# A two-layer decoder trunk on one core: one triangular substitution for two groups of heads, and a new order of steps in the first mixer

## The chip, the core and the metric

The kernel runs on one core of a Trainium2 chip. The core has a matrix engine (TensorE, PE in the profile), a vector engine (VectorE, DVE), a scalar engine (ScalarE, ACT), a general one (GpSimd, POOL) and a queue engine (SyncE, SP) that here only issues DMA transfers. Each engine works through its own instructions in the order in which the built program has them; between engines, semaphores order the work. The metric is the device time of one execution in microseconds (us), lower is better. The kernel before takes 1161.52 us, the median of three runs (1161.10 to 1162.86).

## What is computed

512 tokens of width 1024 go through two layers, each a mixer, a layer norm, a squared-ReLU MLP and a second layer norm. The change lies in the mixer of the first layer:

```python
def mixer_a(h, mem, w_in, conv_w, A_log, dt_bias, norm_w, mem_w_kv, w_o):
    proj = h @ w_in                                  # q, k, v, z, a, b, qm
    qkv = jax.nn.silu(causal_depthwise_conv(qkv, conv_w))
    q, k = l2_normalize(...), l2_normalize(...)      # 6 heads of 128
    o = gated_delta_rule(q, k, v, g, beta)
    o = o * lax.rsqrt(jnp.mean(o * o, axis=-1, keepdims=True) + NORM_EPS) * norm_w
    o = o * jax.nn.silu(z)
    mo = memory_cross_attention(qm, mem, mem_w_kv)   # 4 heads, 256 memory tokens
    return jnp.concatenate([o, mo], axis=-1) @ w_o

def gated_delta_rule(q, k, v, g, beta):              # by chunks of tokens
    L = jnp.where(strict, (k_beta @ k.T) * decay, 0)
    u, w = triangular_solve(I + L, [v * beta, k_beta * exp(g)])
    for each chunk:
        v_new = u - w @ state
        out = q_dec @ state + intra @ v_new
        state = state * chunk_decay + k_dec.T @ v_new
```

## The kernel before

All products are float32 with the operands split into a high and a low part, three matrix products for one (L105 to L107 with the weights as the stationary operand, L118 to L122 with the tokens). A weight slab comes in by one DMA on the SP queue (`wr`, three buffers), ACT casts its high part (L87, `wh`), DVE subtracts for the low part (L88, `wl`); four buffers each.

The six heads form two **groups** of three. The kernel uses chunks of 128 tokens, so a group has 12 units (three heads by four chunks). For each head, k and q are projected (step k, L105), go through the convolution (ACT L385, three DVE instructions L387, ACT's silu L389); then `ak` (L414) makes k·k and k·q, and DVE scales these into `LT` (L427, the triangular matrix) and E (L429, the attention inside a chunk). E's decay matrix is made beforehand by step E from two tiles `y`, one made by DVE and one by POOL (L375).

The inverse of each 128x128 unit triangle is made in two stages. **The substitution** (step i, `inv_blocks`): the 32x32 diagonal blocks of a group's 12 units are gathered through DRAM (`dl` four DMAs, `ld` one), so that 48 partitions hold one block each. 31 steps of two DVE instructions (L483 product `tmp`, L485 subtraction into `X`) invert them all at once; `X` goes back through DRAM (`dx`, then `TT` in four DMAs). **The join** (step j, `inv_join`): DVE transposes TT into `U` (L496), and two levels of small products (32x32: ipp, ip; 64x64: iqp, iq), with copies on ACT and DVE between them, fill the off-diagonal blocks. This is done once per group.

**v** (steps v and w): projection, convolution, then PE transposes (`vt` L459) and DVE scales into `vr` (L460). **z**: step z projects all four token tiles of a column slab (`proj_zMM`), step n applies silu (ACT L686), and POOL multiplies in the norm's weight (L688, 128x768). **The memory's attention** (step m) for one token tile: scores `msc`, DVE's maximum (L619), ACT's exp (L624), transposes `mpt`, copies `pT` (into the buffers named y, which E and the convolutions use too), values `mov`.

**The scan** (step c, `group_chunk`): for one chunk and group kt (transposed k, ACT scales into kd L546), ks and qs (the state with k and q), R on DVE (L555), tr (U times R), vn on ACT (L563), ds (the new state), od, o (ACT L581, DVE L582). Step o (`chunk_out`) squares o on ACT (L592) and multiplies into z. Step f turns a finished token tile into features (L676 to L679), W loads and p applies the output weights (`wo`).

What sets the order: a list of steps, written by hand, is run in this sequence (a letter is the step, digits its arguments; c12 is group 1, chunk 2):

```python
MIXER_ORDER = """q0 g1 g0 E0 k02 k01 k00 E1 k12 i0 k10 k11 q1 z1 m3 v00 i1 m1 w00 v01 j0 m0 v02 w01 m2 z0 w02 M c00 v10 n0 o00
c01 n1 v11 w10 o01 c02 n2 o02 j1 c03 v12 w11 w12 c10 n3 W1 W0 o03 o10 c11 f0 o11 c12 o12 f1 W3 c13 p10 p00 o13
p01 f3 f2 X p11 p02 p12 p03 W2 p23 p20 p30 p32 p31 L0 p21 p13 p22 L1 L2 p33 L3"""
```

A scheduler then lays the instructions of all engines out from it, so that neighbouring steps are interleaved; `behind` puts one instruction behind another on the same engine without a semaphore. The rest of the program (both MLPs, the second layer) comes after and is not touched.

Of the kernel before, what the change touches and what calls it, by code (L numbers as in the profile page):

```python
# [11 lines left out]
F32 = mybir.dt.float32  # L12
# [11 lines left out]
NH = 6  # L24
# [10 lines left out]
MIXER_ORDER = """q0 g1 g0 E0 k02 k01 k00 E1 k12 i0 k10 k11 q1 z1 m3 v00 i1 m1 w00 v01 j0 m0 v02 w01 m2 z0 w02 M c00 v10 n0 o00  # L35
c01 n1 v11 w10 o01 c02 n2 o02 j1 c03 v12 w11 w12 c10 n3 W1 W0 o03 o10 c11 f0 o11 c12 o12 f1 W3 c13 p10 p00 o13
p01 f3 f2 X p11 p02 p12 p03 W2 p23 p20 p30 p32 p31 L0 p21 p13 p22 L1 L2 p33 L3"""
# [12 lines left out]
def trunk(ctx: ExitStack, tc: tile.TileContext, xT, xn, memT, wk, wq, wv, wqm, wz, wmk, wmv, wo0, wo1, up, dn,  # L50
          bw, ws, conv, alog, dtb, nw, sinks, lng, lnb, lngb, pos, invf, out):
    nc = tc.nc
    V, G, A, T, SY = nc.vector, nc.gpsimd, nc.scalar, nc.tensor, nc.sync
# [47 lines left out]
    def feature_major(ps, w, mov_hi, mov_lo):  # L101
        hi, lo = w
        for k in range(KT):
            mh, ml = mov_hi(k), mov_lo(k)
            T.matmul(ps, hi[:, k, :], mh, start=(k == 0), stop=False)  # L105
            T.matmul(ps, hi[:, k, :], ml, start=False, stop=False)
            T.matmul(ps, lo[:, k, :], mh, start=False, stop=(k == KT - 1))  # L107
# [150 lines left out]
    nw_b = row_bcast(nw, P, "nw_b", c0)  # L258
# [34 lines left out]
    def proj_z(zg, gates=None, slabs=None):  # L293

        slabs = slabs or [wload(wz[zg, kh], [P, 4, CW]) for kh in range(2)]
        c0 = zg * CW
        n = min(CW, 768 - c0)
        for t in range(NT):
            ps = mmt("proj_zMM")
            token_major(ps[:, :CW], slabs, x_tok(XH, t), x_tok(XL, t))  # L300
            A.copy(res[:, t, c0:c0 + n], ps[:, :n])
            if gates is not None:
                V.tensor_copy(gates[:, :, t], ps[:, n:n + 12])

    ab = c0([P, 12, NT], "ab")
    slabs = [w[1]() for w in zw]
    for t in range(1, NT):
        xs[t][1](XH[:, :, tok(t)], XL[:, :, tok(t)])
    proj_z(2, ab, slabs)
# [57 lines left out]
    def make_E1(gi):  # L367
        E1 = dt_([P, NU, P], "E1")
        for hl in range(GH):
            h = GH * gi + hl  # L370
            ps = smt("E1")
            psv = ps.rearrange("p (c i) -> p c i", c=4)
            for i, eng in enumerate((V, G)):
                gm = dt_([P, 4, P], "y", dt=F32R)
                eng.tensor_tensor(gm, triu[:, :].unsqueeze(1).broadcast_to([P, 4, P]),  # L375
                                  fr(gsp[i])[:, h * 4:h * 4 + 4].unsqueeze(2).broadcast_to([P, 4, P]), op=ALU.mult)
                T.matmul(ps, slow, gm.rearrange("p c i -> p (c i)"), start=(i == 0), stop=(i == 1))
            dst = E1[:, hl * 4:hl * 4 + 4, :]
            V.tensor_tensor(dst, psv, mtri[:, :].unsqueeze(1).broadcast_to([P, 4, P]), op=ALU.add)
            A.activation(dst, dst, AF.Exp)  # L380
        E1s[gi] = E1

    def conv_silu(ps, ch, dst):
        y = dt_([P, 512], "y")
        A.activation(y, ps, AF.Identity, scale=convw[:, ch, 3:4])  # L385
        for s in (1, 2, 3):
            V.scalar_tensor_tensor(y[:, s:], ps[:, :512 - s], convw[:, ch, 3 - s:4 - s], y[:, s:],  # L387
                                   op0=ALU.mult, op1=ALU.add)
        A.activation(dst, y.rearrange("p (c i) -> p c i", c=4), AF.Silu)  # L389
# [10 lines left out]
    def group_kq(gi, hl):  # L400
# [5 lines left out]
        for which, (wsrc, chb) in enumerate(((wk, 6), (wq, 0))):  # L406
# [3 lines left out]
        ak = [smt("ak").rearrange("p (u i) -> p u i", u=2) for _ in range(2)]  # L410
        ss = dt_([P, 8], "ss")
        junk = dt_([P, P], "junk", bufs=1)
        for c in range(4):
            T.matmul(ak[c // 2][:, c % 2, :], kq[:, hl, c, 0, :], kq[:, hl, c, :, :], start=True, stop=True)  # L414
            V.tensor_tensor_reduce(junk, ak[c // 2][:, c % 2, 0:P], ident, 1.0, 0.0, op0=ALU.mult, op1=ALU.add,
# [8 lines left out]
        for c in range(4):  # L424
            u = hl * 4 + c
            akc = ak[c // 2][:, c % 2, :]
            V.scalar_tensor_tensor(LT[:, u, :], akc[:, 0:P], g["s1"][:, u:u + 1], E1[:, u, :],  # L427
                                   op0=ALU.mult, op1=ALU.mult)
            V.scalar_tensor_tensor(E1[:, u, :], akc[:, P:2 * P], g["rk"][:, u:u + 1], E1[:, u, :],  # L429
                                   op0=ALU.mult, op1=ALU.mult)  # L430
# [12 lines left out]
    def group_v(gi, hl):  # L443
# [5 lines left out]
        conv_silu(ps, 12 + h, g["vt", hl])  # L449

    def group_v2(gi, hl):
        g = groups[gi]
        vt = g["vt", hl]
        if "vr" not in g:
            g["vr"] = dt_([P, GH, 4, P], ("vr", "TT0")[gi], bufs=1)
# [4 lines left out]
        V.tensor_tensor(g["vr"][:, hl], ptv, g["rinv"][:, hl * 4:hl * 4 + 4].unsqueeze(2).broadcast_to([P, 4, P]),  # L460
# [4 lines left out]
    def inv_blocks(gi):  # L465

        LT = groups[gi]["LT"]
        dl = drp.tile([4, NU, 32, 32], F32, tag="dl", name=nm("dl"))
        for b in range(4):
            q = slice(32 * b, 32 * b + 32)  # L470
            SY.dma_start(dl[b].rearrange("u j i -> j u i"), LT[q, :, q])
        ld = dt_([Q, 32, 32], "ld", bufs=1)
        SY.dma_start(ld.rearrange("q j i -> q (j i)"), dl.rearrange("b u j i -> (b u) (j i)"))
        X = dt_([Q, 32, 32], "X", bufs=1)
        G.memset(X, 0.0)
        G.memset(X.rearrange("q i m -> q (i m)")[:, 0:1024:33], 1.0)
        tmp = dt_([Q, 256], "tmp", bufs=1)
        TT = groups[gi]["TT"] = dt_([P, NU, P], f"TT{gi}", bufs=1)
        G.memset(TT, 0.0)
        for j in range(31):  # L480
            n, m = 31 - j, j + 1
            tv = tmp[:, 0:n * m].rearrange("q (i m) -> q i m", m=m)
            V.tensor_tensor(tv, ld[:, j, j + 1:32].unsqueeze(2).broadcast_to([Q, n, m]),  # L483
                            X[:, j, 0:m].unsqueeze(1).broadcast_to([Q, n, m]), op=ALU.mult)
            V.tensor_sub(X[:, j + 1:32, 0:m], X[:, j + 1:32, 0:m], tv)  # L485
        dx = drp.tile([4, NU, 32, 32], F32, tag="dx", name=nm("dx"))
        SY.dma_start(dx.rearrange("b u i m -> (b u) (i m)"), X.rearrange("q i m -> q (i m)"))
        for b in range(4):
            q = slice(32 * b, 32 * b + 32)
            SY.dma_start(TT[q, :, q], dx[b].rearrange("u i m -> i u m"))  # L490

    def inv_join(gi):
        g = groups[gi]
        LT, TT = g["LT"], g["TT"]
        U = g["U"] = dt_([P, NU, P], "U")
        V.transpose(U.rearrange("p u i -> p (u i)"), TT.rearrange("p u i -> p (u i)"))  # L496

        b0, b1, b2, b3 = (slice(32 * b, 32 * b + 32) for b in range(4))
        pp = smt("ipp")[:, 0:NU * 32].rearrange("p (u i) -> p u i", u=NU)
        for u in range(NU):  # L500
            T.matmul(pp[b1, u, :], LT[b0, u, b1], TT[b0, u, b0], start=True, stop=True)
            T.matmul(pp[b3, u, :], LT[b2, u, b3], TT[b2, u, b2], start=True, stop=True)
        Pf = dt_([P, NU, 32], "Pf")
        A.copy(Pf[b1], pp[b1])
        V.tensor_copy(Pf[b3], pp[b3])
        p2 = smt("ip2")[:, 0:NU * 32].rearrange("p (u i) -> p u i", u=NU)
        p3 = smt("ip3")[:, 0:NU * 32].rearrange("p (u i) -> p u i", u=NU)
        for u in range(NU):
            T.matmul(p3[b1, u, :], U[b1, u, b1], Pf[b1, u, :], start=True, stop=True)
        for u in range(NU):  # L510
# [848 lines left out]
```

## Time and profile before

| | |
|---|---|
| median of three runs | 1161.52 us |
| the profiled execution | 1161.59 us, of it 1159.9 us span |
| instructions on the span | 19009 |
| PE, DVE, ACT, POOL busy | 1135.8, 861.0, 555.4, 237.3 us |
| the first mixer's projections to the end of its scan | about 50 to 270 us of the span |

Busy time of an engine is the union of its instructions. A matmul in the profile has a modelled end, so that matmuls which follow each other overlap: how fast PE really works is read from the distance of their starts.

### The profile page before, as it was taken

The numbers are of one execution on the slowest core, as the hardware profiler recorded it, in microseconds if no ns is written. First come the engines' busy times: TensorE is split into PE (matmuls) and PEld (weight loads), VectorE is DVE, ScalarE is ACT, GpSimd is POOL, SyncE is SP. The second block draws the span as 40 slices with busy tenths as digits, with TensorE's granted clock in tenths as the row PEclk, the third lists the DMA queues.
The fourth block names the chain that finished last, engine by engine and source line by source line (L and its number), as shares of the span: only waits on it lengthen the run. The fifth ranks groups of instructions, "written<-read, shape, count | busy, mean of one in ns | idle before, by whom it ended". The sixth has DMA issues, their size and how long they took to land.

```text
span 1159.9 us, 19009 instructions
## 1 busy us (share of the span) xinstructions
PE 1135.8 (98%) x7494; PEld 1000.2 (86%) x7494; DVE 861.0 (74%) x1612; ACT 555.4 (48%) x1010; POOL 237.3 (20%) x178
## 2 busy tenths in 40 slices
PE   9999999989999999999999999999999999999997
PEld 9887788879998899898988887778989898989986
DVE  5678889867798766667675968886987667676657
ACT  6445354755484445444443336661655444444531
POOL 1202111110014332424220100000042324233203
PEclk9999999999999999999999999999999999999999
DMA  8523041204323233242323241102333242322311
GB/s 297 163 74 89 34 137 38 68 20 158 129 76 126 94 98 121 73 135 84 122 96 107 63 140 56 56 20 73 110 118 119 75 137 81 124 95 91 128 37 73
DMA packets 41017, 114.17 MB, mean 98 GB/s; under 512 B 11168, under 2 KB 12064, under 8 KB 40928
## 3 DMA queue, kind: packets, MB, share of 16 engines
q1 hardware_dynamic: 40496, 112.17, 29.6%
q8 instruction: 59, 0.97, 0.3%
q10 hardware_dynamic: 432, 0.79, 0.2%
q14 instruction: 30, 0.25, 0.1%
HBM read 109.53 MB, written 3.41 MB: 97 GB/s over the span
## 4 chain that ended last, share of the span: by engine, by line
PE 81%; DVE 13%; ACT 3%; issue 1%; POOL 1%; DMA 0%; SPq 0%; DVEq 0%; ACTq 0%; POOLq 0%
PE dn L121 10%; PE dn L122 10%; PE dn L118 10%; PE upb L949 3%; PE upb L951 3%; PE upb L950 3%; PE wo L122 2%; PE wo L118 2%; PE wo L121 2%; PE upd L951 2%; PE upd L950 2%; PE upd L949 2%; PE upa L950 2%; PE upa L951 2%; PE upa L949 2%; DVE y L387 2%
## 5 line engine op out<-in xcount | busy, mean ns | idle before, releaser
L87 ACT CAST wh<-wr 128x1024 fp32r<-128x1024 f32 (+1 forms) x126 | 132.2, 1052 | 213.0 <-PE dn L122 153.2
L88 DVE TENSOR_TENSOR wl<-wr,wh 128x1024 fp32r<-128x1024 f32 (+1 forms) x126 | 153.9, 1224 | 65.2 <-ACT wh L87 64.8
L118 PE MATMUL dn<-wh,hh 128*128 128x512 f32 (+1 forms) x516 | 200.3, 388 | 0.0
L122 PE MATMUL dn<-wh,hl 128*128 128x512 f32 (+1 forms) x516 | 200.3, 388 | 0.0
L121 PE MATMUL dn<-wl,hh 128*128 128x512 f32 (+1 forms) x516 | 200.2, 388 | 0.0
L122 PEld LDWEIGHTS dn<-wh,hl 128*128 128x128 f32 x516 | 96.9, 188 | 19.9
L121 PEld LDWEIGHTS dn<-wl,hh 128*128 128x128 f32 x516 | 97.0, 188 | 18.9
L118 PEld LDWEIGHTS dn<-wh,hh 128*128 128x128 f32 x516 | 97.0, 188 | 18.8
L1030 DVE TENSOR_TENSOR res<-res,dn 128x512 f32<-128x512 f32 (+1 forms) x121 | 82.0, 678 | 40.9 <-PE dn L122 40.8
L939 POOL TENSOR_TENSOR sa<-wr 128x512 f32<-128x512 f32 x26 | 35.5, 1367 | 353.7 <-DMA wr<-in_up_dram 326.3
L728 POOL TENSOR_TENSOR rs<-rs,nhalf 128x1 f32<-128x1 f32 x16 | 12.8, 799 | 324.7 <-DVE rs L727 271.3
L949 PE MATMUL upb<-TH,wh 128*128 128x256 f32 x208 | 57.6, 277 | 1.6 <-DVE u L988 1.6
L950 PE MATMUL upa<-XL,wh 128*128 128x256 f32 x208 | 57.7, 278 | 0.0
L940 POOL TENSOR_TENSOR sb<-sa,wr 128x512 f32<-128x512 f32 x26 | 57.7, 2220 | 0.0
L951 PE MATMUL upa<-XH,wl 128*128 128x256 f32 x208 | 57.6, 277 | 0.0
L127 DVE TENSOR_TENSOR hl<-r,hh 128x1024 fp32r<-128x1024 f32 x26 | 56.1, 2159 | 1.9 <-ACT hh L126 1.9
L951 PE MATMUL upd<-XH,wl 128*128 128x256 f32 x208 | 57.5, 276 | 0.0
L951 PE MATMUL upb<-TH,wl 128*128 128x256 f32 x208 | 57.5, 276 | 0.0
L949 PE MATMUL upd<-XH,wh 128*128 128x256 f32 x208 | 57.5, 276 | 0.0
L950 PE MATMUL upb<-TL,wh 128*128 128x256 f32 x208 | 57.5, 276 | 0.0
L950 PE MATMUL upd<-XL,wh 128*128 128x256 f32 x208 | 57.5, 276 | 0.0
L126 ACT CAST wh<-wr 128x1024 fp32r<-128x1024 f32 x26 | 27.4, 1054 | 53.6 <-PE upa L950 53.6
(410 smaller groups left out, 3314.9 us busy)
## 6 DMA issues: line engine op xcount, KB each, us to landing
wr<-in_up_dram SPq DMA_DIRECT2D x64, 512.0 KB, 4.4
wr<-in_dn_dram SPq DMA_DIRECT2D x64, 512.0 KB, 4.4
wr<-in_wo_dram SPq DMA_DIRECT2D x16, 512.0 KB, 3.7
wr<-in_bw_dram SPq DMA_DIRECT2D x8, 512.0 KB, 4.2
wr<-in_wk_dram SPq DMA_DIRECT2D x6, 512.0 KB, 3.7
wr<-in_wq_dram SPq DMA_DIRECT2D x6, 512.0 KB, 4.1
wr<-in_wv_dram SPq DMA_DIRECT2D x6, 512.0 KB, 3.7
wr<-in_wz_dram SPq DMA_DIRECT2D x4, 520.0 KB, 4.4
```

Of the source, the lines that this page charges most:

```text
L87: A.copy(hi, raw)
L88: V.tensor_sub(lo, raw, fr(hi))
L118: mm = T.matmul(ps, sh, hi[:, kk, :], start=(k == 0), stop=False)
L121: T.matmul(ps, sh, lo[:, kk, :], start=False, stop=False)
L122: last = T.matmul(ps, sl, hi[:, kk, :], start=False, stop=(k == nk - 1))
L127: return V.tensor_sub(lo, src, fr(hi))
L939: G.tensor_tensor(sa[:, 0], raw[1][:, kA], raw[1][:, kB], op=ALU.add)
L940: G.tensor_tensor(sb[:, 0], sa[:, 0], raw[0][:, kA], op=ALU.subtract)
L949: T.matmul(ps, hi[:, k, :], m, start=start and k == 0, stop=False, skip_group_check=True)
L950: T.matmul(ps, hi[:, k, :], ml[:, k, :], start=False, stop=False, skip_group_check=True)
L951: T.matmul(ps, lo[:, k, :], mh[:, k, :], start=False, stop=stop and k == 3, skip_group_check=True)
L1030: V.tensor_tensor(dst, dst, ps, op=ALU.add)
```

## The change

1. The substitution runs once for both groups: 96 partitions, 31 steps. Each head's blocks are gathered as soon as that head's `LT` exists (`inv_gather`, step i with two digits, four DMAs a head), each group's into its half of `ld`; step I is the substitution, J the two transposes into U, j the join of both groups, whose levels alternate between the groups. The second copy of `Pf` moves from DVE to ACT.
2. `ak` is two products: k·k after k's projection and q·k after q's.
3. The memory's attention is three steps (m scores, t turn, u values) and stands among the projections of k and q; both qm projections come first. `pT` uses the buffer of X.
4. z is projected one token tile at a time (step y), after the slab's load (step z); the norm's weight is no longer multiplied by POOL (L688 goes) but as a scale on ACT and DVE where a finished tile is turned into features.
5. The scan's step c ends with vn, and d (`group_state`) does the rest, so that the chunks of both groups alternate. The squares of a chunk stand behind the next chunk's vn, and f behind the next R.
6. The convolutions of v's heads 3 and 4 stand behind the last substitution step, that of head 5 behind the transposes into U.

```diff
-MIXER_ORDER = """q0 g1 g0 E0 k02 k01 k00 E1 k12 i0 k10 k11 q1 z1 m3 v00 i1 m1 w00 v01 j0 m0 v02 w01 m2 z0 w02 M c00 v10 n0 o00
...
+MIXER_ORDER = """E02 g0 q0 g1 q1 E01 k02 i02 m0 t0 E12 E00 k01 u0 k12 i12 m1 t1 i01 m2 k00 E11 t2 u1 i00 E10 m3 k10 t3
+u2 i10 u3 k11 v00 w00 i11 v01 v02 w01 z1 I y10 z0 y11 J y12 y13 w02 y00 y01 v10 v11 n0 v12 w10 y03 y02 j w11 c00 w12 n1
+c10 d00 d10 c01 n2 W1 d01 c11 W0 d11 o00 o10 c02 c12 n3 d12 f0 d02 o01 o11 p10 W3 c03 o02 f1 c13 p11 d03 d13 o12 p00 f2
...
-        conv_silu(ps, 12 + h, g["vt", hl])
+        conv_silu(ps, 12 + h, g["vt", hl], None if h < 3 else diag["last"] if h < 5 else diag["U"])
...
+    def inv_gather(gi, hl):
...
+            SY.dma_start(dl[b, u4].rearrange("u j i -> j u i"), g["LT"][q, u4, q])
+        g["moved"] += 1
+        if g["moved"] == GH:
+            SY.dma_start(diag["ld"][gi * Q:gi * Q + Q].rearrange("q j i -> q (j i)"),
+                         dl.rearrange("b u j i -> (b u) (j i)"))
...
-            V.tensor_tensor(tv, ld[:, j, j + 1:32].unsqueeze(2).broadcast_to([Q, n, m]),
-                            X[:, j, 0:m].unsqueeze(1).broadcast_to([Q, n, m]), op=ALU.mult)
-            V.tensor_sub(X[:, j + 1:32, 0:m], X[:, j + 1:32, 0:m], tv)
...
+            V.tensor_tensor(tv, ld[:, j, j + 1:32].unsqueeze(2).broadcast_to([2 * Q, n, m]),
+                            X[:, j, 0:m].unsqueeze(1).broadcast_to([2 * Q, n, m]), op=ALU.mult)
+            diag["last"] = V.tensor_sub(X[:, j + 1:32, 0:m], X[:, j + 1:32, 0:m], tv)
...
+        for f, i in ((lower, 0), (lower, 1), (upper, 0), (lower, 2), (upper, 1), (lower, 3), (upper, 2), (upper, 3)):
+            f(i)
...
+    def group_state(gi, c):
...
+        if c:
+            qs = v3(smt("qs"))
             for hl in H:
                 T.matmul(qs[:, hl, :], kq[:, hl, c, 1, :], St[:, hl, :], start=True, stop=True)
...
-            A.activation(junk, o[:, hl, :], AF.Square, accum_out=sso[:, hl:hl + 1])
+            behind(A.activation(junk, o[:, hl, :], AF.Square, accum_out=sso[:, hl:hl + 1]), g.get(("vn", c + 1)))
...
-        zv = res[:, t, 0:768].rearrange("p (h d) -> p h d", h=NH)
-        G.tensor_tensor(zv, zv, nw_b[:, :].unsqueeze(1).broadcast_to([P, NH, P]), op=ALU.mult)
...
-        to_features(res[:, t, :], t)
+
+        for j in range(2):
+            features_half(res[:, t, :], t, j, nw_c, 4 - 2 * j, mmt)
```

What this makes of the order is seen in three places. The first is DVE where group 1's substitution begins in the kernel before (tmp and X are the substitution, y a head's convolution, v its projection, mx the maximum of the attention's scores, wl a weight's low part):

```order
331 L485 TENSOR_TENSOR X_1215<-X_1215,tmp_1218 48x31
332 L88 TENSOR_TENSOR wl_2119<-wr_2116,wh_2118 128x1040
333 L387 SCALAR_TENSOR_TENSOR y_1714<-v_1682,convw,y_1714 128x511
334 L619 TENSOR_REDUCE mx_1807<-msc_1801 128x2
335 L387 SCALAR_TENSOR_TENSOR y_1714<-v_1682,convw,y_1714 128x510
336 L619 TENSOR_REDUCE mx_1807<-msc_1802 128x2
337 L387 SCALAR_TENSOR_TENSOR y_1714<-v_1682,convw,y_1714 128x509
338 L620 TENSOR_SCALAR mx_1807<-mx_1807 128x4
339 L483 TENSOR_TENSOR tmp_1730<-ld_1725,X_1727 48x31
340 L485 TENSOR_TENSOR X_1727<-X_1727,tmp_1730 48x31
```

In the changed kernel DVE comes to the one substitution here (L539 and L541 are its two lines, L416 the convolution, L109 a weight's low part):

```order
253 L416 SCALAR_TENSOR_TENSOR y_1712<-v_1680,convw,y_1712 128x509
254 L481 SCALAR_TENSOR_TENSOR rq_74_703<-ss_1604 128x4
255 L482 TENSOR_SCALAR rqs_704<-ss_1604 128x4
256 L539 TENSOR_TENSOR tmp_1827<-ld_865,X_1824 96x31
257 L506 TENSOR_TENSOR vr_1718<-vt_1719,rinv_658 128x512
258 L541 TENSOR_TENSOR X_1824<-X_1824,tmp_1827 96x31
259 L109 TENSOR_TENSOR wl_1933<-wr_1930,wh_1932 128x1040
260 L416 SCALAR_TENSOR_TENSOR y_1762<-v_1730,convw,y_1762 128x511
```

The maxima are gone from this place, and the first substitution step, which waits for `ld`, now has a weight's subtraction and the convolution of the second v head (`v_1730`) right behind it.

The second is SP's queue in the changed kernel, where the last heads' blocks are gathered (`dl_1167` is group 1's DRAM tile, `ld_865` the tile that the substitution reads):

```order
53 L521 DMA dl_1167<-LT_76_705 32x4x32 x4
54 L105 DMA wr_1936<-in_wz_dram 128x1040
55 L521 DMA dl_1167<-LT_76_705 32x4x32 x4
56 L105 DMA wr_2083<-in_wv_dram 128x1024
57 L524 DMA ld_865<-dl_1167 48x1024
58 L105 DMA wr_2121<-in_wv_dram 128x1024
```

In the kernel before it stands so, for group 0:

```order
43 L471 DMA dl_1208<-LT_72_695 32x12x32 x4
44 L84 DMA wr_1555<-in_wz_dram 128x1040
45 L473 DMA ld_1213<-dl_1208 48x1024
46 L84 DMA wr_1683<-in_wv_dram 128x1024
```

Both put one weight load between the gather and `ld`; the gather that counts is now that of one head instead of a whole group.

The third is PE at the end of the join. Before, for group 1 (v is the last head's projection, the rows below it group 0's last chunk and v's transposes):

```order
1176 L521 MATMUL iqp_2573<-TT_225_1731,LT_63_686 64x64 x6
1177 L105 MATMUL v_2633<-XH,wh_2636 128x512
1178 L106 MATMUL v_2633<-XL,wh_2636 128x512
1179 L107 MATMUL v_2633<-XH,wl_2637 128x512
1180 L526 MATMUL iq_350_2582<-U_2502,Pf_2580 64x64 x6
1181 L521 MATMUL iqp_2590<-TT_225_1731,LT_63_686 64x64 x6
1182 L526 MATMUL iq_353_2599<-U_2502,Pf_2597 64x64 x6
1183 L553 MATMUL ks_2607<-S_2268,kq_687 128x128 x3
1184 L558 MATMUL qs_2608<-S_2268,kq_687 128x128 x3
```

In the changed kernel, for both groups, and on into the first chunks:

```order
1040 L69 MATMUL iq_318_2413<-U_1968,Pf_2402 64x64 x6
1041 L69 MATMUL iqp_2421<-TT_266_1830,LT_76_705 64x64 x6
1042 L69 MATMUL iq_321_2430<-U_1968,Pf_2411 64x64 x6
1043 L69 MATMUL iqp_2438<-TT_266_1830,LT_76_705 64x64 x6
1044 L69 MATMUL iq_324_2447<-U_1970,Pf_2428 64x64 x6
1045 L69 MATMUL iq_325_2455<-U_1970,Pf_2445 64x64 x6
1046 L72 MATMUL vt_2463<-ident,vt_2151 128x128 x4
1047 L72 MATMUL kt_2471<-ident,kq_656 128x128 x3
1048 L69 MATMUL tr_2478<-vr_1718,U_1968 128x128 x3
1049 L72 MATMUL vt_2485<-ident,vt_2190 128x128 x4
1050 L72 MATMUL kt_2494<-ident,kq_697 128x128 x3
1051 L69 MATMUL tr_2501<-X_2197,U_1970 128x128 x2
```

No projection stands among the join's products any more, and the first chunks of both groups follow at once; the first output-weight products come two chunk pairs later.

282 lines of the change are left out of this document (171 added, 111 removed).

## The prediction, as put on record

> **What bounds the kernel now.** First the page's busy times, then its chain of work:
>
> ```profile
> PE 1135.8 (98%) x7494; PEld 1000.2 (86%) x7494; DVE 861.0 (74%) x1612; ACT 555.4 (48%) x1010; POOL 237.3 (20%) x178
> ...
> PE 81%; DVE 13%; ACT 3%; issue 1%; POOL 1%; DMA 0%; SPq 0%; DVEq 0%; ACTq 0%; POOLq 0%
> ```
>
> PE is the bound, and its matmuls stay as they are but for details. So only two things can be won: time in which PE has nothing to start, and time at a lower clock. Two neighbouring starts from PE's timeline give the pace:
>
> ```profile
> 60.11 0.39 PE L105 MATMUL kq<-XH,wh 128*128 128x512 f32 x1
> 60.34 0.39 PE L106 MATMUL kq<-XL,wh 128*128 128x512 f32 x1
> ```
>
> A 512-wide matmul takes 0.227 us of PE, though it is shown as 0.39. From the starts of all matmuls, each less its usual distance (about 0.11 us for 128 columns), I get the **gaps**, which are more than the idle time. The windows view of the first mixer, with its columns of busy time and count:
>
> ```profile
> core 0: us, PE busy (x) PEld busy (x) DVE busy (x) ACT busy (x) POOL busy (x), PEclk, DMA share, GB/s
> 50.00:150.00 100.00, 96.93 (x455) 77.80 (x454) 82.12 (x238) 45.52 (x100) 19.48 (x17) 1.00 0.24 73
> 150.00:210.00 60.00, 56.72 (x485) 47.51 (x483) 53.92 (x130) 32.41 (x60) 10.05 (x8) 1.00 0.23 68
> 210.00:237.00 27.00, 26.36 (x180) 23.41 (x181) 21.50 (x52) 18.73 (x54) 1.70 (x2) 1.00 0.26 74
> 237.00:247.00 10.00, 8.71 (x182) 7.10 (x182) 6.83 (x17) 4.84 (x12) 0.85 (x1) 1.00 0.18 56
> 247.00:250.60 3.60, 3.60 (x18) 3.54 (x18) 2.77 (x6) 0.88 (x3) 0.00 (x0) 0.53 0.00 0
> 250.60:270.00 19.40, 17.72 (x142) 16.29 (x141) 13.32 (x42) 14.16 (x54) 2.54 (x3) 1.00 0.11 32
> ```
>
> By the starts these six rows hold gaps of 7.6, 8.1, 2.8, 3.3, 2.3 and 3.4 us: **27.5 us**. That is all the change can reach; the rest of the span has no part in it. The fifth row is a stretch at half clock (0.53). The waits of PE name the larger gaps:
>
> ```profile
> PE vt L459 <- ACT vt L389: 2.4, 2, 1.8
> ...
> PE E L377 <- POOL y L375: 1.3, 2, 1.1
> PE ak L414 <- ACT kq L389: 1.3, 2, 1.0
> ...
> PE ds L567 <- ACT LT L563: 1.1, 2, 0.6
> PE proj_zMM L118 <- DVE y L387: 0.8, 1, 0.8
> ...
> PE iq L526 <- DVE U L515: 0.7, 1, 0.7
> PE iq L526 <- ACT Pf L523: 0.6, 1, 0.6
> PE proj_zMM L118 <- ACT res L301: 0.5, 1, 0.5
> ```
>
> How the longest comes about stands in the timeline of all engines before it:
>
> ```profile
> 202.82 1.87 POOL L688 TENSOR_TENSOR res<-res,nw_b 128x768 f32<-128x768 f32 x1 [7.33 <-ACT res L686]
> ...
> 202.93 1.99 DVE L485 TENSOR_TENSOR X<-X,tmp 48x207 f32<-48x207 f32 x1
> ...
> 205.34 0.35 DVE L485 TENSOR_TENSOR X<-X,tmp 48x192 f32<-48x192 f32 x1
> ...
> 207.07 1.85 POOL L688 TENSOR_TENSOR res<-res,nw_b 128x768 f32<-128x768 f32 x1 [2.38 <-ACT res L686]
> ...
> 207.55 1.54 DVE L483 TENSOR_TENSOR tmp<-ld,X 48x156 f32<-48x156 f32 x1
> ...
> 210.47 0.66 PE L459 MATMUL vt<-ident,vt 128*128 128x128 f32 x4 [1.85 <-ACT vt L389]
> ```
>
> A substitution step takes 0.35 us alone and 1.5 to 2.0 us beside POOL's multiplication; the convolution behind it comes late, then ACT's silu, then PE's transposes.
>
> **The change part by part.** Its own figures are not the gain: they lie on DVE, beside PE.
>
> ```profile
> L387 DVE SCALAR_TENSOR_TENSOR y<-kq,convw,y 128x511 f32<-128x511 f32 (+2 forms) x36 | 26.5, 741 | 6.1 <-ACT y L385 5.9
> L483 DVE TENSOR_TENSOR tmp<-ld,X 48x31 f32<-48x31 f32 (+15 forms) x62 | 24.2, 390 | 2.4 <-POOL X L476 1.8
> L485 DVE TENSOR_TENSOR X<-X,tmp 48x31 f32<-48x31 f32 (+15 forms) x62 | 22.0, 355 | 0.6
> ```
>
> One substitution instead of two saves half of 24.2 + 22.0, **23.1 us of DVE**; twice the partitions should not lengthen a step, since its elements per partition stay. POOL's four multiplications go too. What PE makes of it goes by stages; each is given as gaps after, against gaps before.
>
> *Projections of k and q, now with the attention among them: 8.0.* Before, the 7.6 of the first row, and of the 8.1 of the second some 2 that belong to the attention's small products (8.1 less 2.7 at the two vt, 1.6 at z and 1.9 in group 0's join). They move along: 9.6. E's wait of 1.3 should go, since E is now made head by head and early; the waits of ak stay, in the split form. DVE loses group 0's substitution from this stage and gets the attention's maxima, copies and results, some 14 us against 10, so its share (82.12 of 100) hardly changes. Bounds: 5 where both E and ak stop waiting, 13 where DVE, in which nothing is left that nobody waits for, delays each of the six heads by a further 0.8.
>
> *v and z: 3.0.* The waits at vt and z (4.3 of gaps) lose their cause with POOL's multiplication and with z by token tiles. But a new wait comes. In the kernel before the substitution's first step came so long after the last LT:
>
> ```profile
> 106.03 0.35 DVE L427 SCALAR_TENSOR_TENSOR LT<-ak,s,E 128x128 f32<-128x128 f32 x1
> ...
> 117.22 0.17 DVE L483 TENSOR_TENSOR tmp<-ld,X 48x31 f32<-48x31 f32 x1
> ```
>
> These 10.8 us are the way through DRAM, which is as long for one head. After the last head's LT, DVE has some 6.5 us of work ahead of the first step (four convolution pieces at 0.74, four E at 0.34, a low part at 1.2), so it stands about 4 us, and the convolution of v's second head is queued behind. Counted from that head's ak: LT at 6, first step at 16.9, the step, a low part, vr and three pieces 4.7, silu 0.6: PE's vt at 22.2. PE itself has 79 wide matmuls (17.9) and 1.9 of small ones, 19.8. **The stall is 2.4**; bounds 0 (the blocks land 3 us sooner) and 5. To it 0.6 of small gaps. From the first step DVE needs 23.1, five low parts (6.1), two convolutions (4.4) and vr (1.8): 35.4. X then leaves and returns:
>
> ```profile
> dx<-X SPq DMA_DIRECT2D x2, 192.0 KB, 4.7
> TT<-dx SPq DMA_DIRECT2D x8, 48.0 KB, 2.3
> ```
>
> With four issues between, about 9 us: TT at 61.3. PE, behind vt, has eight z tiles (24 x 0.12 each), three v (5.45 each) and two vt, 40.2: it comes to the join at 62.8. Only 1.5 us of cover; each us beyond that costs one.
>
> *The joins: 1.6.* Before, 3.3 and 1.9. One group's copies now lie beside the other's products; what is left is the first copy of Pf, which nothing covers now that no projection stands there.
>
> *Half clock: 2.3, as before.* It came in the stretch behind a join with 8.71 of 10 us busy; the new join has more tiny products in a row. Bounds 0 and 4.6 (two stretches). The Trainium skill, "TensorE: Matmul & The Clock Gate", Part 1 and "Why this matters for your kernels", lets the clock fall after a window of 3.4 us without PE activity, and asks for no gap above some 3 us. Here the stretch came though PE waited for no more than 0.7 us at once (iq), so the row speaks against the rule as I read it; by the rule alone, none of my gaps reaches 3 us, and this is rival E.
>
> *The scans: 6.0.* Before 2.8 + 3.4, with group 0's chunks among v's projections. ACT's part of a chunk:
>
> ```profile
> L592 ACT ACTIVATE junk<-LT 128x128 f32<-128x128 f32 x20 | 6.2, 312 | 2.4 <-DVE LT L582 2.1
> L563 ACT ACTIVATE LT<-tr,brk 128x128 f32<-128x128 f32 x21 | 6.2, 370 | 1.6 <-PE tr L561 1.6
> L546 ACT ACTIVATE LT<-kt,kds 128x128 f32<-128x128 f32 x18 | 5.6, 364 | 4.2 <-PE kt L544 4.2
> L581 ACT ACTIVATE LT<-qs,gate 128x128 f32<-128x128 f32 x15 | 4.7, 373 | 5.4 <-PE qs L558 3.6 <-DVE res L602 1.8
> ...
> L592 ACT ACTIVATION_READ_ACCUMULATOR junk<-LT 128x1 f32 x20 | 3.9, 193 | 0.0
> ```
>
> Three of each: 4.8 us for a chunk of a group, 9.7 for a pair. PE has 66 starts at 0.11, 7.3 us. The first two pairs have no output weights to fill in: by durations ACT is longer by 2.8 (first pair, without o) and 2.4. Neighbouring ACT instructions overlap, so I take 3.5 of 5.2, and 2.5 for the turns between tiles. Bounds 4 and 9. Costing nothing: the split of ak (48 products half as wide), the scale that replaces POOL's product (within existing casts), Pf's copy on ACT. The sixteen further DMAs of the gathers sit on SP ahead of weight loads that wait for a buffer anyway; without that cover they would hold back a weight by some 2 us a head.
>
> Sum: 8.0 + 3.0 + 1.6 + 2.3 + 6.0 = 20.9 against 27.5, **6.6 us less**. The profiled execution took 1161.59, 0.07 above the median: 1155.0.
>
> **The rivals.**
>
> *A, the first stage takes it back.* The attention's DVE and ACT work is now among instructions that PE waits for within microseconds, and PE has three banks to run ahead. For it: in the first row every large gap is such a wait. Against it: DVE's share there does not grow. At 13 plus a stall of 5 at vt, the sum is 27.9: 1162.
>
> *B, no gain because the 23.1 us of DVE was cover all along.* For it: PE is 98% busy. Against: the vt and z waits. If only 2 us of them go: 1160.
>
> *C, slower: the half clock lasts through the joins and the first two pairs.* It is one stretch of some 26 us, in which no wide product stands: 10.8 of joins (by the starts in the fourth row one group's 168 tiny products take 4.6, two groups' 9.2, and 1.6 of gaps) and 15.4 of chunks (11.9 of starts and 3.5). At half clock the joins grow by 7.6 (9.2 doubled, less the 10.8), the pairs from ACT's 15.4 to 23.8, 8.4; less the 2.3 counted, +13.7: **1168.7**. It decides where some two thirds of that stretch run at half clock (8.8 us more than forecast, 1163.8). For it, the fifth row; against it, that before the clock came back by 250.6 among chunks.
>
> *D, more is won.* If E, ak and the new vt wait all vanish and the scans pack, 13 us of gaps stay: 1147.
>
> *E, no half clock at all.* For it: before, the clock fell behind one join of two only, and there PE had waited at iq twice, where the staggered levels now wait less. Against it: the new stretch of tiny products is longer. Its price is the 2.3 alone: 1152.7.
>
> **How the numbers follow.** The forecast, 1150.5 to 1159.2 with a stretch of half clock, gets 0.40, E 0.13; A 0.14, B 0.08, C 0.13, D 0.12. A range from 1147 to 1165 leaves out D's lower half and most of C, about 0.17. A measurement of this kernel can tell about 0.2%, 2.3 us, from no change. Faster by more than that: 0.40 + 0.13 + 0.12 and a third of A and B, 0.07: 0.72. Within: 0.14. Slower: C and a little of A, 0.14.
>
> **What the profile will show.** Right: 31 pairs of substitution steps, each near 0.35 us; PE waiting for the second v head's vt by 2 to 3 us behind a DVE that waits for `ld`; no wait ahead of ipp; one or two windows at 0.5 clock in the join or the first pairs. Wrong: a wait of PE for TT (the chain is longer), waits of more than 1 us at each kq or ak (A), a mean clock near 0.6 over the joins and first pairs (C). The largest unknown is the first stage, where my gaps are carried over rather than worked out.

## The result, and the profile after

The changed kernel takes 1169.35 us, the median of four runs (1167.42 to 1170.75), against 1161.51 for the kernel before on the same chip: a ratio of 1.0063, 95% interval 1.0051 to 1.0075. It is **slower by 7.3 us** by that ratio, 7.8 by the medians; the forecast was 1155.0, in a range that ended at 1165.

The page of the changed kernel, its span, busy times and chain of work ("issue" is time in which an engine waited for nothing that the profile shows):

```profile
span 1168.0 us, 19067 instructions
...
PE 1147.0 (98%) x7542; PEld 1014.2 (87%) x7542; DVE 840.7 (72%) x1552; ACT 554.9 (48%) x1014; POOL 228.7 (20%) x172
...
PE 85%; DVE 8%; ACT 3%; issue 2%; POOL 1%; DVEq 0%; ACTq 0%; POOLq 0%
```

The change did what it says: DVE works 20.3 us less, POOL 8.6 us less, and DVE's share of the chain falls from 13% to 8%. But PE is busy 11.2 us *more*. Where, is told by one tile, `dn`, the second product of both MLPs, with its first and last start (duration as least/median/most, in ns). In the kernel before:

```profile
L118 PE MATMUL dn<-wh,hh x516: 278/389/481, 355.6 to 1151.7; 128*128 128x512 f32 x170, 128*128 128x256 f32 x2
```

In the changed kernel:

```profile
L69 PE MATMUL dn<-wh,hh x516: 278/389/487, 353.3 to 1159.8; 128*128 128x512 f32 x170, 128*128 128x256 f32 x2
```

Up to the first `dn` the changed kernel is ahead by 2.3 us. From the first to the last, in code that the change doesn't touch, it takes 806.5 us in place of 796.1: **10.4 us lost there**. The MLPs' first product is made for 26 pairs of weight slabs, each in seven groups of twelve 256-wide products, into the tiles `upa`, `upb` and `upd`. The page's rows of it name the instructions (mean ns of one stands behind the comma). Before:

```profile
L950 PE MATMUL upa<-XL,wh 128*128 128x256 f32 x208 | 57.7, 278 | 0.0
...
L951 PE MATMUL upd<-XH,wl 128*128 128x256 f32 x208 | 57.5, 276 | 0.0
L951 PE MATMUL upb<-TH,wl 128*128 128x256 f32 x208 | 57.5, 276 | 0.0
```

After:

```profile
L69 PE MATMUL upd<-XH,wl 128*128 128x256 f32 x208 | 58.5, 281 | 0.0
L69 PE MATMUL upa<-XL,wh 128*128 128x256 f32 x208 | 58.4, 281 | 0.0
...
L69 PE MATMUL upb<-TH,wl 128*128 128x256 f32 x208 | 58.1, 279 | 0.0
```

Three to five nanoseconds look like nothing, and the overlap hides how much they are: by the distance of their starts, these 256-wide products follow each other every 113.3 ns before (114.8 in the first group of a pair) and every 117.7 to 118.3 after. There are 2184 of them: 2184 x 4.5 ns = 9.8 of the 10.4 us. `dn` itself keeps its 227 ns.

What can change the pace of untouched instructions? The change replaces the norm weight's broadcast `nw_b`, 512 bytes a partition in another pool, by `nw_c`, one float a partition, in the pool `cp`. The MLPs' tiles that are allocated behind it now lie 32 bytes higher in the on-chip memory. What the first product reads, in bytes of a partition, as the built programs have it:

```
           before   after
x0         116352   116384    (moved)
TH          91552    91584    (moved)
TL         103840   103872    (moved)
w2h        118496   118528    (moved; with w2l the weights of upb's third group)
XH, XL, the other weights' wh and wl, and dn's hh, hl   (not moved)
```

`upb` streams TH and TL, `upa` and `upd` stream XH and XL, and only the very first product of each pair of weight slabs reads `x0`, a copy of a piece of XH.

The mixer itself, by the windows view of the changed kernel (PE's busy time and count first, the granted clock third from the end):

```profile
core 0: us, PE busy (x) PEld busy (x) DVE busy (x) ACT busy (x) POOL busy (x), PEclk, DMA share, GB/s
50.00:157.60 107.60, 104.81 (x558) 83.96 (x557) 77.78 (x210) 58.20 (x129) 20.00 (x17) 1.00 0.23 69
157.60:217.50 59.90, 59.90 (x366) 52.90 (x364) 50.92 (x116) 24.64 (x41) 2.97 (x4) 1.00 0.31 92
217.50:234.40 16.90, 14.72 (x343) 14.27 (x342) 10.41 (x14) 7.62 (x14) 0.00 (x0) 0.63 0.16 55
234.40:250.00 15.60, 14.54 (x118) 13.80 (x117) 8.66 (x25) 10.11 (x40) 0.85 (x1) 0.96 0.00 1
250.00:270.00 20.00, 18.83 (x152) 17.45 (x150) 15.22 (x55) 14.01 (x57) 3.36 (x4) 1.00 0.16 54
```

The five rows hold gaps of 9.6, 1.2, 7.3, 2.8 and 3.5 us, 24.4 in all against 27.5 before: 3.1 won where 6.6 were forecast. The third row, the joins, is at 0.63 of the clock; by the clock's records it was halved for 13.65 us, from 221.9 on. PE's waits in the mixer:

```profile
PE ip L69 <- issue: 2.0, 1, 2.0
PE E L69 <- DVE y L403: 0.9, 1, 0.9
PE tr L69 <- DVE LT L632: 0.7, 2, 0.4
PE ak L69 <- ACT kq L419: 0.6, 2, 0.4
...
PE E L69 <- POOL y L403: 0.4, 1, 0.4
```

### The profile page after: what moved, and what is told of

It reads as the page before. It is cut to its first block, busy times and chain, and to the rows that moved or that the text cites. A ratio compares the mean times of both kernels' runs of the same rounds, so it can differ in the third digit from the quotient of the medians.

```text
span 1168.0 us, 19067 instructions
## 1 busy us (share of the span) xinstructions
PE 1147.0 (98%) x7542; PEld 1014.2 (87%) x7542; DVE 840.7 (72%) x1552; ACT 554.9 (48%) x1014; POOL 228.7 (20%) x172
## 4 chain that ended last, share of the span: by engine, by line
PE 85%; DVE 8%; ACT 3%; issue 2%; POOL 1%; DVEq 0%; ACTq 0%; POOLq 0%
PE dn L69 29%; PE upb L69 9%; PE wo L69 6%; PE upd L69 6%; PE upa L69 6%; PE kq L69 4%; PE projqMM L69 3%; PE proj_zMM L69 3%; PE v L69 3%; PE up L69 3%; PE ov L69 1%; PE ssc L69 1%; DVE wl L109 1%; PE VM L69 1%; PE KM L69 1%
## 5 line engine op out<-in xcount | busy, mean ns | idle before, releaser
L109 DVE TENSOR_TENSOR wl<-wr,wh 128x1024 fp32r<-128x1024 f32 (+1 forms) x126 | 154.0, 1223 | 67.9 <-ACT wh L108 67.8
```

Source lines behind the costliest of these rows:

```text
L109: V.tensor_sub(lo, raw, fr(hi))
```

## The experiments: the MLPs' pace

**Is it the 32 bytes?** The kernel before gets one idle float ahead of what moved, and the changed kernel gets `nw_c` where a pad (a filler tile that nothing uses) gave way to it, so that no tile of the MLPs moves.

```diff
 (e1_before_shift, on the kernel before)
     nw_b = row_bcast(nw, P, "nw_b", c0)
+    ct([P, 1], "pad_nw")
 (e2_after_noshift, on the changed kernel)
-    ct([P, 56], "pad1")
+    ct([P, 48], "pad1")
+    nw_c = ct([P, 1], "nw_c")
```

> The kernel before with one unused 4-byte tile where the change puts nw_c, so that all that is allocated behind it lies 32 bytes higher; the order of every engine is as before. Theory A (addresses: the MLPs' 256-wide matmuls go at 118 ns instead of 113 because the tiles they read moved by 32 bytes): some 1171, upa, upb and upd near 118 ns, first dn where it was (about 355.6 us). Rival B (PE's own stream: 21 more PE instructions and other PSUM banks in the change set the pace): 1161.5, all at 113.

> The changed kernel with nw_c put into the space of an existing pad, so that what lies behind has the addresses of before; nothing else. Theory A: upa, upb, upd back at 113 ns, some 10 us less than the changed kernel, 1159 (the mixer's gain of 2.3 us alone is left). Rival B: 1169, still 118 ns.

e1 took 1173.70 us, ratio to before 1.0092 (1.0076 to 1.0109); e2 took 1157.96, ratio 0.9958 (0.9943 to 0.9972). e2's row of `dn`:

```profile
L69 PE MATMUL dn<-wh,hh x516: 278/389/487, 352.9 to 1148.3; 128*128 128x512 f32 x170, 128*128 128x256 f32 x2
```

795.4 us, as before the change; in e1 it is 806.6 (356.8 to 1163.4). So the loss lies wholly in the shift, and without it the change is faster by 4.9 us (0.0042 of 1162.49).

**Which tile?** First `x0` alone, 32 bytes lower on the kernel before (e3) and 32 higher on the changed one (e4); then TH and TL alone, 32 higher on the kernel before (e5).

```diff
 (e3_before_x0; e4_after_x0 makes it 48 and 16)
-            pool.tile([P, 40], F32, tag="pad3", name=nm("pad3"), bufs=1)
+            pool.tile([P, 32], F32, tag="pad3", name=nm("pad3"), bufs=1)
...
-            pool.tile([P, 24], F32, tag="pad4", name=nm("pad4"), bufs=1)
+            pool.tile([P, 32], F32, tag="pad4", name=nm("pad4"), bufs=1)
 (e5_before_thtl; TH and TL are allocated between)
+            pool.tile([P, 8], F32, tag="pad5", name=nm("pad5"), bufs=1)
...
-            pool.tile([P, 16], F32, tag="pad2", name=nm("pad2"), bufs=1)
+            pool.tile([P, 8], F32, tag="pad2", name=nm("pad2"), bufs=1)
```

> The kernel before with only the tile x0 (the first moving operand of each upa) 32 bytes lower, by two pads around it that keep all else in place. Theory A1 (x0's place alone sets the pace of all the products behind it): about 1171, upa, upb, upd at 118. Theory A2 (each product's own operands set its pace): upa's first product alone changes, under 0.2 us in all, 1161.5. Rival B: 1161.5.

> The changed kernel with only x0 moved, 32 bytes up, all else as in the change (TH, TL, w2h stay 32 bytes off their place of before). Theory A1: upa and upd back at 113, some 6 to 10 us less than the changed kernel, 1159 to 1163; upb may stay slower, since its own tiles are still moved. Theory A2: no change, 1169: upa and upd do not read x0 but once. Rival B: 1169.

> The kernel before with the tiles TH and TL of both MLPs alone moved by 32 bytes (a pad of 8 floats ahead of them, taken off the pad behind them); every other tile keeps its place. Theory 'TH and TL set the pace': they are what upb multiplies, and the slow pace is theirs: upb goes from 113 to 118 ns from start to start (936 x 4.6 ns = 4.3 us, about 1166), and if it carries over to upa and upd too, all three do (about 1171 to 1172). Rival 'another of the moved tiles': all three stay at 113 and the time is that of before, 1161.5.

e3: 1161.54, ratio 0.9994 (0.9984 to 1.0003). e4: 1168.37, 1.0050 (1.0034 to 1.0066). So `x0` alone, at these two places, neither brings the loss nor takes it away. e5: 1170.62, 1.0075 (1.0058 to 1.0092): moving TH and TL is enough for most of it, 804.1 us from the first `dn` to the last where the kernel before has 796.1 and the changed one 806.5. And it slows `upa` and `upd` too, which don't read them. How, is seen in e5's timeline of PE (start, shown duration) from one group of twelve to the next:

```profile
413.50 0.28 PE L952 MATMUL upa<-XH,wl 128*128 128x256 f32 x1
413.62 0.28 PE L950 MATMUL upa<-XH,wh 128*128 128x256 f32 x1
413.73 0.28 PE L951 MATMUL upa<-XL,wh 128*128 128x256 f32 x1
413.84 0.28 PE L952 MATMUL upa<-XH,wl 128*128 128x256 f32 x1
413.96 0.28 PE L950 MATMUL upb<-TH,wh 128*128 128x256 f32 x1
414.07 0.28 PE L951 MATMUL upb<-TL,wh 128*128 128x256 f32 x1
414.19 0.28 PE L952 MATMUL upb<-TH,wl 128*128 128x256 f32 x1
...
415.37 0.28 PE L950 MATMUL upa<-XH,wh 128*128 128x256 f32 x1
415.49 0.28 PE L951 MATMUL upa<-XL,wh 128*128 128x256 f32 x1
415.61 0.28 PE L952 MATMUL upa<-XH,wl 128*128 128x256 f32 x1
415.73 0.28 PE L950 MATMUL upa<-XH,wh 128*128 128x256 f32 x1
415.84 0.28 PE L951 MATMUL upa<-XL,wh 128*128 128x256 f32 x1
```

The first `upa` ends at steps of 0.113 us, `upb` goes at some 0.118, and the second `upa`, which streams the same XH and XL as the first, stays at 0.118. The stream has two paces here and keeps the one it is in.

**Is the pace really carried?** e11 moves nothing. It only lets the first product of each pair read XH where it is, and not the copy `x0`.

```diff
-                product(self.a, self.A11, xq["B11"], True, False, xq["first"])
+                product(self.a, self.A11, xq["B11"], True, False)
```

> The kernel before with nothing moved: only the first product of each pair's first group (upa) reads its first slice of x from XH, where it is, and not from its copy x0; the copy is still made. Theory P, 'the matmuls stream in one of two paces, 113 or 118 ns, and keep the one that they are in until a product from an unfavourable place throws them out of it' (in e5_before_thtl the first upa runs at 114.8, the next group, on the moved TH and TL, at 117.8, and all groups behind it at 117.8 to 118.2, though upa and upd read nothing that was moved): the first upa starts at 118 behind dn; all groups stay there if the places of TH and TL keep a pace and don't restore it (about 1170), or only the first upa is slow if they restore it (26 pairs x 12 x 4 ns = 1.2 us, about 1162.5). Rival 'each group's pace is its own operands' place': 113 ns everywhere behind the first product, 1161.5.

1171.39 us, ratio 1.0079 (1.0060 to 1.0097), and its row:

```profile
L118 PE MATMUL dn<-wh,hh x516: 277/389/478, 357.4 to 1161.4; 128*128 128x512 f32 x170, 128*128 128x256 f32 x2
```

804.0 us: one product in 84 changed its source, and all seven groups of the 84 became slower (the last row of the table below). The pace is carried; that each group's pace is its own operands' matter is refuted.

**Which places are good?** e6 is e1 with TH and TL 32 bytes higher still, e7 the kernel before with the shift made 64 bytes, e12 the kernel before with TH and TL alone 128 bytes higher.

```diff
 (e7_before_shift64; e6_shift_but_thtl is e1 and e5 together)
+    ct([P, 9], "pad_nw")
 (e12_before_thtl128; pad3 goes, so x0 stays in its place)
+            pool.tile([P, 32], F32, tag="pad5", name=nm("pad5"), bufs=1)
...
-            pool.tile([P, 16], F32, tag="pad2", name=nm("pad2"), bufs=1)
+            pool.tile([P, 24], F32, tag="pad2", name=nm("pad2"), bufs=1)
```

> The kernel before with everything behind the constants moved by 32 bytes (as in e1_before_shift, 1173.7) and TH and TL by 32 more, so that they lie at an odd multiple of 32 bytes again, as in before. Theory 'TH and TL set the pace': the fast pace is back, 113 ns, about 1162. Rival 'another of the moved tiles': 118 ns stays, about 1173.

> The kernel before with everything behind the constants moved by 64 bytes where e1_before_shift moved it by 32. Theory 'the place modulo 64 bytes decides': all tiles keep their remainder, 113 ns, about 1161.5. Rival 'any other place is worse' (the places of before are a find of their own): 118 ns, about 1173; or another pace between.

> The kernel before with TH and TL alone moved by 128 bytes (e5_before_thtl: by 32, slow; all by 64 was slow too). Theory 'the place modulo 128 bytes decides': 113 ns, 1161.5. Rival 'the place of before is one of few': 117 to 120 ns in upb and behind it, 1166 to 1172.

e6: 1170.68, ratio 1.0081 (1.0066 to 1.0096). e7: 1170.16, 1.0074 (1.0059 to 1.0089). e12: 1166.69, 1.0041 (1.0028 to 1.0054). No rule by 64 or 128 bytes holds; e6's result was neither of the two expected. The median of the mean pace, in ns, by a group's position in a pair (26 pairs, twelve products a group) tells more than the sums:

```
                 x0      TH     upa   upb   upa   upb   upd   upb   upd
before, e2     116352  91552   114.8 113.3 113.3 113.3 113.3 113.3 113.3
e3             116320  91552   114.8 113.3 113.3 113.3 113.3 113.3 113.3
changed, e1    116384  91584   117.8 118.2 117.8 118.2 118.1 118.3 117.7
e4             116416  91584   118.1 118.5 117.8 118.2 118.1 118.3 117.8
e5             116352  91584   114.8 117.8 117.8 118.2 117.8 118.2 117.8
e6             116384  91616   117.8 119.4 114.9 118.4 115.2 118.1 114.3
e7             116416  91616   118.2 119.9 114.6 118.4 115.2 117.5 114.9
e12            116352  91680   114.8 117.8 113.9 117.8 113.9 117.8 113.9
e11            not read 91552  117.8 117.8 117.8 117.8 117.8 117.8 117.8
```

`x0`'s place decides the first group, TH's the others: at 91552 `upb` keeps either pace, at 91584 it makes the stream slow for good, at 91616 and 91680 it is slow itself (119.4 and 119.9 where it first comes in e6 and e7, slower than either pace) and `upa` and `upd` recover behind it. In the changed kernel both tiles left a good place. Why these places and no others stays open.

## The experiments: the joins

The other term that missed is the joins' 7.3 us with 13.65 us at half clock. Two theories: PE's stall inside `ip` (2.0 us, by "issue", behind 96 products of `ipp` and some 120 of `ip` in 4.4 us) starts it; or the array does too little work. For the second I count **full columns**: columns times the share of the 128x128 array in use (a 32x32x32 product is 2, a 128x512 is 512), in windows of 3.413 us, in whose multiples the clock changes.

e8 sets two z tiles among the tiny products of e2:

```diff
-... n0 v12 w10 y03 y02 j w11 c00 w12 n1
+... n0 v12 w10 j y03 y02 w11 c00 w12 n1
```

> The changed kernel without the move of 32 bytes (e2_after_noshift, 1157.96) with the two last z tiles of the upper half put behind the step j, so that the scheduler may set their 512-wide products among the tiny ones of the substitution's product and joins. Theory I 'the stall of 1.4 to 2.0 us ahead of ip starts the half clock': with long products among the tiny ones PE does not run out, no slice at half clock in the joins, and 4 of the 13.65 us at half clock that the tiny products lose, and more, come back: about 1152 to 1154. Theory II 'the long stretch of tiny products itself is enough': the half clock stays, and only the stall goes: 1156 to 1157.5. Rival: the tiles come too early for their inputs and PE waits in their place: 1158 or more.

1154.19 us, ratio 0.9942 (0.9927 to 0.9957): the best kernel here, faster than both. In three of its four runs the mean granted clock, the share of the full clock over the whole span, is 0.998 or 0.999; in one, 1156.68 us, it is 0.993, as in e2. The trace is of a run at 0.998; its windows through the joins:

```profile
214.00:218.00 4.00, 4.00 (x92) 3.64 (x92) 1.19 (x2) 1.56 (x4) 0.00 (x0) 1.00 0.68 252
218.00:222.00 4.00, 4.00 (x91) 3.68 (x93) 3.08 (x3) 2.83 (x6) 0.00 (x0) 1.00 0.02 4
222.00:226.00 4.00, 3.73 (x107) 3.55 (x105) 2.96 (x5) 2.99 (x5) 0.00 (x0) 1.00 0.02 4
226.00:230.00 4.00, 3.79 (x62) 3.59 (x57) 3.40 (x6) 1.83 (x4) 0.00 (x0) 1.00 0.38 121
```

No half clock in this run and no stall, so the two theories are not yet apart. e9 puts 14 idle products of 256 columns among the tiny ones of e2; e10 puts one z tile among `iqp` and `iq` and leaves `ipp` and `ip` bare; e13 is e9 with 512 columns.

```diff
 (e9_fill_joins, also for ip2, ip3, iqp and iq2; e13_fill_512 writes ps from XH[:, 0, :])
+        def filled(n):
+            ps = smt(n)
+            T.bar()
+            T.matmul(ps[:, 0:256], XH[:, 0, 0:P], XH[:, 0, 0:256], start=True, stop=True)
+            T.bar()
+            return ps
-            pp = smt("ipp")[:, 0:NU * 32].rearrange("p (u i) -> p u i", u=NU)
+            pp = filled("ipp")[:, 0:NU * 32].rearrange("p (u i) -> p u i", u=NU)
 (e10_z_in_iq, at the end of lower and upper's loop)
+            if (f, i) == (lower, 1):
+                T.bar()
+                z_tile(0, 2)
+                T.pin = None
```

> The kernel of e2_after_noshift (1157.96) with 14 idle products of 128x256 (XH by itself) in the joins, one ahead of each piece ipp, ip2, ip3, iqp and iq2, written into the piece's own PSUM tile and then written over; nothing of the result changes. They cost 14 x 0.118 = 1.65 us of PE. Theory W, 'the clock is halved after a window of 3.41 us in which the array did little work' (columns times the share of the array in use: in the traces so far the windows ahead of a half clock hold at most 832 full columns, save two of e5_before_thtl, those ahead of a full one at least 866): with the fillers every window of the joins holds over 1,300, so no half clock in the joins at all, iqp and iq at 58 ns in place of 106, 96 x 48 ns = 4.6 us less, and about 1155 to 1156.5 in all. Theory I, 'PE's stall ahead of ip starts it': if a stall of about 1 us is still there, the half clock is too, 10 to 14 us long, and the time is 1158 to 1160.

> The kernel of e2_after_noshift with the z tile (0,2), 24 products of 128x260, set inside the joins behind the second piece of iqp; ipp and ip stay as they are, one behind the other with nothing between. Theory W (work of the array in a window): the window with the tail of ipp and with ip holds a few hundred full columns, so the half clock begins there as in e2, at the same place, but ends in the window behind the z tile's: 3.4 to 7 us in place of 13.65, and about 1156 to 1157. Theory I (a stall starts it and it lasts as long as the tiny products do): the stall of 1.4 us is still there, half clock 10 to 14 us, about 1158.

> As e9_fill_joins (1166.5, half clock of 23.9 us from the window behind one with 1,036 full columns), with 14 idle products of 128x512 in place of 128x256: 14 x 0.227 = 3.2 us of PE over e2_after_noshift. Over all traces so far a window of 3.41 us with under 850 full columns was always followed by half clock, one with over 1,900 never, and between them it went either way. Theory W (work of the array): the fillers bring the windows of the joins to about 2,000, so no half clock there, iqp and iq at 58 ns, and 1157 to 1160. Rival (the tiny products themselves, however many, not the work): the half clock is there again, over 10 us long, and 1164 or more.

e9 went against both: 1166.53 us, ratio 1.0041 (1.0026 to 1.0056). No wait of PE is listed in the joins, and yet the half clock lasts 23.9 us, longer than ever:

```profile
214.00:218.00 4.00, 4.00 (x92) 3.69 (x93) 2.23 (x3) 3.37 (x5) 0.00 (x0) 1.00 0.67 250
218.00:222.00 4.00, 4.00 (x129) 3.54 (x122) 3.61 (x6) 3.12 (x6) 0.00 (x0) 0.80 0.42 135
222.00:226.00 4.00, 4.00 (x76) 3.59 (x73) 1.72 (x3) 0.61 (x2) 0.00 (x0) 0.50 0.01 4
226.00:230.00 4.00, 4.00 (x27) 3.28 (x26) 0.22 (x1) 1.45 (x3) 0.00 (x0) 0.50 0.00 0
230.00:234.00 4.00, 4.00 (x27) 3.28 (x26) 1.72 (x3) 0.47 (x1) 0.00 (x0) 0.50 0.00 0
```

The stall is out as a cause: the clock fell at 220.4 us with none before it. The trace of e13, with the same instructions and longer fillers, has no half clock there:

```profile
222.00:226.00 4.00, 4.00 (x98) 3.28 (x98) 2.65 (x5) 1.02 (x3) 0.00 (x0) 1.00 0.01 4
226.00:230.00 4.00, 4.00 (x44) 3.00 (x42) 1.68 (x2) 1.58 (x3) 0.00 (x0) 1.00 0.00 0
230.00:234.00 4.00, 4.00 (x43) 3.05 (x42) 1.17 (x3) 0.47 (x1) 0.00 (x0) 1.00 0.01 4
```

It took 1158.59 us, the median, 7.9 us less than e9 with 1.6 us more of fillers; the ratio, 0.9986, leaves open whether it is faster than the kernel before (0.9950 to 1.0022). One of its four runs took 1167.78 at a mean granted clock of 0.989, as low as e9's four (0.987 to 0.990), where the other three have 0.998 or 0.999: the longer fillers kept the clock up in three runs of four. e10 took 1157.79, 0.9963 (0.9950 to 0.9976): half clock for 10.2 us where 3.4 to 7 were expected, to the end of the window that holds the z tile, and no stall by "issue". Full columns by window, with ">" where the clock is halved behind a window and "<" where it comes back:

```
before    2836  1820   832 >  2048 <
changed   5312   314 >  118   624   672  1456 <
e2        2298   208 >  454   688   832  2048 <
e8        5024  1794  3784   866  1568  3968
e9        6044  1036 >  912   592   816   832   640  1216  2048 <
e10        246 >  158   412  3428 <
e13       3548  2224  1480  2000  2080
```

Over the fifteen traces no window under 850 was followed by the full clock, and none over 1,900 by the half as long as products followed (at the program's end, where PE's work stops within a window, 2,048 in e6 and e11 and 2,304 in e7 were); between, both came (1,036 and 1,360 halved, e5 even after 1,636 and 1,852, while 866 and 1,062 stayed full). So the work of the array fits best, with a threshold that these counts blur. Plain columns, without the share in use, do not fit: e9's window ahead of the fall has 5,056 of them, and one of e12's that stayed at the full clock 3,008. A count by the share of the array's rows alone sorts the windows as well (always halved up to 1,408, never above 2,320), so which measure of work it is stays open. e9's fillers brought 1,036 where I had worked out over 1,300; that half the work fits into a window once the clock is halved, and that this keeps it there, agrees with its windows but was not tested apart.

How long the half clock lasts also differs between runs of the same work. Eight traces here have the first mixer of the kernel before, instruction for instruction: five of them have 3.4 us at half clock (before, e1, e3, e6, e7), two have 10.2 (e5, e11) and one none (e12). The windows do not start with the program: in the fifteen traces their edges lie at other places of it from run to run, so the same tiny products are cut differently. One trace does not size this term.

## Why the prediction was wrong

**The step that failed** is the one ahead of the sum: "PE is the bound, and its matmuls stay as they are but for details", and "That is all the change can reach; the rest of the span has no part in it". The change reached 2184 matmuls in the rest, at 4.5 ns each, by moving what some of them read: TH and TL for `upb`, `x0` for one product in 84; the others took over the pace. The prediction counted the removal of POOL's product and the scale in its place among the edits "costing nothing"; the tile that came with it, 32 bytes in the layout, cost 10.4 us. It forecast 6.6 us of gain, the trace shows 2.3 up to the MLPs, less 10.4: the span went from 1159.9 to 1168.0.

The terms themselves, as gaps in us; e2 is the same mixer without the shift, e8 that with two z tiles among the joins:

| term | forecast | changed | e2 | e8 |
|---|---|---|---|---|
| k, q and the attention | 8.0 | 9.6 | 8.4 | 9.3 |
| v and z | 3.0 | 1.2 | 0.8 | 1.7 |
| joins and half clock | 1.6 + 2.3 | 7.3 | 7.1 | 2.2 |
| scans | 6.0 | 6.3 | 7.0 | 6.1 |
| sum | 20.9 | 24.4 | 23.3 | 19.3 |

- *k, q and the attention*: E's wait "should go" and didn't, 0.9 and 0.4 in the rows above. The prediction's own terms give 8.3 (9.6 less 1.3) and not 8.0. Rival A, this stage taking everything back, did not come.
- *v and z*: the stall of 2.4 at `vt` is absent. The substitution's steps took what was assumed, 0.36 us in the median with twice the partitions. I had 10.8 us from the end of the last LT to the first step, the way through DRAM taken to be as long for one head as for a group; DVE's timeline of the changed kernel has 7.3 (162.69 to 169.98), and `ld` held DVE for 0.3 only:

```profile
161.57 1.12 DVE L466 SCALAR_TENSOR_TENSOR LT<-ak,s,E 128x128 f32<-128x128 f32 x4
...
169.98 0.19 DVE L539 TENSOR_TENSOR tmp<-ld,X 96x31 f32<-96x31 f32 x1 [0.32 <-DMA ld<-dl]
```

- *Joins and half clock*: the term of the sum that was mis-sized most, 3.9 against 7.3. The clock was halved for 13.65 us and not for one window, and products of 64 columns came 106 ns apart in place of 58 (96 x 48 ns = 4.6 us); the stall of 2.0 us for "issue" was not foreseen. The forecast took the half clock from the one trace of before, 3.4 us long; the same mixer has between none and 10.2 in eight traces. e8 shows that the term could be 2.2.
- *Scans*: 6.0 against 6.3, right.
- *Rival C* named 1168.7, near the result, by another way: its half clock was to last through the first two pairs, some 26 us, and did not. The number is an accident.
- With the shift taken out, 4.9 us were won (e2) of the 6.6 that were forecast. e2's gaps are 2.4 us over the sum: the joins 3.2, the scans 1.0 and the first stage 0.4 more, v and z 2.2 less. The chance of 0.14 for slower was too small for another reason as well: no rival left the mixer.

The rule weighed in the prediction, the Trainium skill's "TensorE: Matmul & The Clock Gate", Part 1, ties the clock to how busy PE has been and to idle windows. e9's rows disagree with the profile's busy time as the measure: 4.00 of 4 us busy from 214 on, the clock halved at 220.4, and then 4.00 of 4 us busy at 0.50.

## What to carry to other kernels

When a change adds, drops or resizes a tile, list the places of all tiles before and after, and look at the distance of the starts of untouched matmuls: a few ns on thousands of them outweigh a stage that was won by hand. Put a new tile where a pad can give way to it, then judge the change. Stretches of tiny products want long products among them: here, while products followed, no window of 3.4 us with over 1,900 full columns led to half clock. And read the granted clock of every run, not of the traced one alone.

## What was not expected of the hardware

- A stream of 256-wide products has two main paces, 113.3 and 117.8 ns, and keeps one over groups whose operands differ: one product's source in 84 switched all (e11), 32 bytes in TH's place switched them for good (e5), 128 bytes only while TH was read (e12). The Trainium skill, "TensorE: Matmul & The Clock Gate", "Back-to-back issue gap", gives one figure for a width, 262 cycles at 256, for the gap of an isolated matmul (an estimate by its 2.4 GHz: 109 ns), and lets weight loads and matmuls together set the spacing of a stream. The traces here, a stream with a weight load for each product, show two paces, both above that figure.
- Behind some 215 products of 32x32 in 4.4 us PE stood for 2.0 us that the profile puts to "issue"; 1.4 in e2, 0.7 in e4, none with fillers between (e9), and none in e10, where the same products stood bare but PE waited 0.9 and 0.7 us for ACT and DVE between them. What holds PE there stays open.
- The clock fell with PE busy all the time (e9), and stayed down for seven windows.
